# A hybrid encoder trunk on one core: the first loads reordered and halved, one memset for the warm-up, the last products by token halves

## The chip, the core and the metric

The kernel runs on one core of a Trainium2 chip. A core has TensorE (PE, matrix products; PEld is its weight load), VectorE (DVE), ScalarE (ACT), GpSimd (POOL) and SyncE (SP), which here only issues DMAs. The metric is device microseconds of one execution. The kernel before took 1095.82 us, the median of three runs (1095.76 to 1098.31).

## What is computed

Two residual layers over 512 tokens of 1024 features. Layer 0 mixes tokens with a bidirectional gated linear attention, layer 1 with grouped-query softmax attention; each is followed by a gated feed-forward part with a width-3 convolution. An RMS norm stands ahead of each of the four. All inputs and outputs are float32. The stages that the change touches are the first products of layer 0 and the last of layer 1:

```
h = rmsnorm(x, norm_mix[0])
proj = h @ w_in                          # q, k, v, g, r
r_f, r_b = split(r)                      # rank 16 each
log_decay = log_sigmoid(r_dir @ w_up + b_up) / 16
...
x = x + conv_ffn(rmsnorm(x, norm_ffn[1]), ...)   # ends in (silu(gate) * val) @ w_down
```

## The kernel before

**Layout and arithmetic.** `x` is held with features on the partitions: eight chunks `x[c]` of 128 x 512, two to a tile. Every float32 product is three products of a faster type: each operand is split into `hi` (ACT writes a copy, L247 for weights, L373 for inputs) and `lo` (DVE subtracts, L248 and L378), and PE adds `hi*hi`, `hi*lo` and `lo*hi` in one PSUM bank. The RMS factor of a token is multiplied in after the product, so that PE needs only `x` times the norm's weight, not the sums of squares, to begin. Those sums are formed beside (`square`, L380 to L386).

**The beginning.** ACT loads the parameter table `prm` (L302). SP issues 16 DMAs of 256 KB in turn (L307, L308): `x[0]`, the weights of chunk 0, `x[1]`, the weights of chunk 1, and so on. At most eight DMAs are on their way for SP: the ninth waits until the first has landed. DVE fills the two halves of the tile `two` (L320, L321), and eight small products of it (L324) keep PE at work while the loads are under way; what they sum to becomes `halfneg`, the constant -0.5 that an exponent needs later (L326). `gla` then takes `norm.high(0)`, the split of the first weights, whose first half is copied by DVE (L245) and not ACT, and `norm.low(0)` (L488 to L492). The first projection, `seg(0)`, runs `token_steps` (L426 to L444): for each chunk of features there are four token blocks `j`, each with its own PSUM bank, and three products for each. For the first two chunks the products are sorted by operand (L436): four `hi*hi`, then four with the weights' `lo`, then four with the inputs' `lo`. From the third chunk on they go block by block.

**Between.** The sums of squares are turned to token factors `rtok` (L389 to L398), with one step on POOL. PE computes the gate input `rp` (L541) and spreads `rtok` over columns (L349); DVE copies that to `R` (L404) and forms `rf = rp*R` (L545); ACT copies it to `rst` (L547) and DVE corrects 32 of its rows (L548). The gate weights `gst` are copied by ACT (L536) and 32 rows of them corrected by POOL (L537). Products `z` of `gst` and `rst` (L559) stand in PE's order among the products of the second projection `seg(1)`: the first `z` comes after 24 of them. A weight half is brought to SBUF by SP (L169), and copied by ACT into one of four `wh` buffers, of which one holds the gate input's weights `rw` until PE has read them.

**The order.** The code is recorded, and a scheduler sets the order in which the instructions of each engine stand; each engine then works through its own list in order, waiting on semaphores. A small edit can thus move instructions that it doesn't name.

**The end.** The last 24 steps of the list `PLAIN` (L1065 to L1073) sum the last four output chunks, six steps of three products each for a chunk, with all 512 tokens in one PSUM bank. `end` (L1028) adds the bank to `x[c]` on DVE and stores it; for the last chunk it does so by token halves, the first stored through SP, the second through ACT's queue (L1036 to L1038).

Of the kernel before, what the change touches and what calls it, by code (L numbers as in the profile page):

```python
# [8 lines left out]
F32 = mybir.dt.float32  # L9
F32R = mybir.dt.float32r  # L10
U8 = mybir.dt.uint8
AF = mybir.ActivationFunctionType
ALU = mybir.AluOpType

P = 128
S = 512
D = 1024
KC = D // P
NT = S // P
# [5 lines left out]
FC = DFF // P  # L25

SEG_BANKS = (("acc", "acc", "pt", "pt"), ("s", "s", "acc", "acc"), ("acc", "pt", "pt", "s"), ("s", "acc", "acc", "acc"))


GATE_STEPS, GATE_LAG = (1, 3, 5, 7, 10, 12, 15, 17), 2  # L30


# [9 lines left out]
NQ, NPART = 4, 2  # L42
PLAIN = ([(c, k) for c in range(4) for k in range(16, 20)] + [(c, k) for c in range(4) for k in (20, 21)]
         + [(c, k) for c in range(4, 8) for k in range(16, 22)])
# [28 lines left out]
def hybrid_encoder_kernel(  # L73
# [20 lines left out]
    pe, act, dve, pool, sync = nc.tensor, nc.scalar, nc.vector, nc.gpsimd, nc.sync  # L94
    mm = pe.matmul
# [14 lines left out]
    def bank(tag, n):  # L110
        return pp.tile([P, S], F32, tag=tag, bufs=PS[tag], name=nm(n))

    def pair(tag, bufs, dt, n):
        return sp.tile([P, 2 * S], dt, tag=tag, bufs=bufs, name=nm(n))

    def big(dt, n):
        return pair("g", 22, dt, n)

    def tmp(tag, n, w=S):
        return sp.tile([P, w], F32, tag=tag, bufs={"u": 3, "t": 5, "sq": 3}[tag], name=nm(n))  # L120
# [5 lines left out]
    x, x_home = [], []  # L126
# [177 lines left out]
    raw = [pair("raw", NR, F32, "first") for i in range(4)]  # L304
    for c in range(KC):
        r = slice((c % 4) * S, (c % 4 + 1) * S)
        sync.dma_start(x[c], xT[c * P : (c + 1) * P, :])  # L307
        sync.dma_start(raw[c // 2][:, (c % 2) * S : (c % 2 + 1) * S], w_vg[c // 4, :, r])  # L308
    for n in range(4):
        W.loaded[id(w_vg), n // 2, n % 2] = raw[n]  # L310

# [6 lines left out]

    two = tmp("u", "two")
    dve.memset(two[:, :P], 2.0 ** -5)  # L320
    dve.memset(two[:, P : 2 * P], -(2.0 ** -6))  # L321
    warm = bank("po", "warm")
    for i in range(8):
        mm(warm[:, :P], two[:, :P], two[:, P : 2 * P], start=i == 0, stop=i == 7)  # L324
    halfneg = cp.tile([P, 8], F32, name="halfneg")
    dve.tensor_copy(halfneg, warm[:, :8])  # L326
    ones = cp.tile([P, 1], F32, name="ones")
    dve.memset(ones, 1.0 / D)
    bd = cp.tile([P, 2], F32, name="bd")
# [22 lines left out]
    class Norm:  # L352
# [15 lines left out]
        def weight(self, c):  # L368
            return prm[:, PC_NORM + self.idx * KC + c : PC_NORM + self.idx * KC + c + 1]

        def high(self, c):
            t = pair("xhl", 8, F32R, "xhl")
            act.activation(t[:, :S], x[c], AF.Copy, scale=self.weight(c))  # L373
            self.hl[c] = (t[:, :S], t[:, S:])

        def low(self, c):
            hi, lo = self.hl[c]
            dve.scalar_tensor_tensor(lo, x[c], self.weight(c), hi.bitcast(F32), ALU.mult, ALU.subtract)  # L378

        def square(self, c):  # L380
            q = tmp("sq", "sq")
# [24 lines left out]
    def mm3(ps, wh, wl, mh, ml, start, stop):  # L406

        mm(ps, wh, mh, start=start, stop=False)  # L408
        mm(ps, wh, ml, start=False, stop=False)  # L409
        return mm(ps, wl, mh, start=False, stop=stop)  # L410
# [15 lines left out]
    def token_steps(src, i0, hl, ps, width, per_half):  # L426

        for hf in range(KC // per_half):
            wh, wl = W.half(src, i0 + hf)

            late = src is w_vg and i0 > 0 and hf == 0
            for kk in range(per_half):
                todo = [(kk, j, i) for j in range(NT - late) for i in range(3)]
                if late and kk == 1:
                    todo += [(k, NT - 1, i) for k in range(2) for i in range(3)]
                if src is w_vg and i0 + hf * per_half + kk < 2:  # L436
                    todo.sort(key=lambda a: a[2])
                for a, j, i in todo:
                    k, sl = hf * per_half + a, slice(a * width, (a + 1) * width)
                    mm(ps[j][:, :width], hl[k][i == 2][:, j * P : (j + 1) * P], (wl if i == 1 else wh)[:, sl],  # L440
                       start=k == 0 and i == 0, stop=k == KC - 1 and i == 2)
                if kk == 1:
                    W.flush()
                yield  # L444

    def token_tiles(*a):
        for _ in token_steps(*a):
            pass
# [38 lines left out]
    def gla(norm, nxt):  # L487
# [10 lines left out]
        def seg(i, between=None):  # L498
            ps = [bank(tag, "vg") for tag in SEG_BANKS[i]]
            for n, _ in enumerate(token_steps(w_vg, i * 4, norm.hl, ps, S, 2)):  # L500
                if between is not None:
                    between(n)
            return ps
# [318 lines left out]
    def ffn(layer, norm, cw, nxt):  # L822
# [4 lines left out]
        plain = {}  # L827
# [102 lines left out]
        H = S // 2  # L930
# [97 lines left out]
        def end(c, ps):  # L1028
            if nxt is not None or c < KC - 1:
                dve.tensor_tensor(x[c], x[c], ps, ALU.add)  # L1030
                if nxt is not None:
                    nxt.chunk(c)
                else:
                    sync.dma_start(out[c * P : (c + 1) * P, :], x[c])
            else:
                for sl, queue in ((slice(0, S // 2), sync), (slice(S // 2, S), act)):  # L1036
                    dve.tensor_tensor(x[c][:, sl], x[c][:, sl], ps[:, sl], ALU.add)
                    queue.dma_start(out[c * P : (c + 1) * P, sl], x[c][:, sl])  # L1038
# [3 lines left out]
        for m in range(FC):  # L1042
# [15 lines left out]
            else:  # L1058
                for i, y in enumerate(held):
                    t = big(F32R, "gu")  # L1060
# [3 lines left out]
        cur, open_ = None, {}  # L1064
        for u, (c, k) in enumerate(PLAIN):  # L1065
            if u % 8 == 0:
                cur = W.half(w_dn, NPART * NQ * 2 + u // 8)
            sl = slice((u % 8) * P, (u % 8 + 1) * P)
            if c not in open_:
                open_[c] = bank("s" if c == 3 else "acc", "dn")  # L1070
            mm3(open_[c], cur[0][:, sl], cur[1][:, sl], *plain[k], k == 2 * NQ * NPART, k == FC - 1)
            if k == FC - 1:
                end(c, open_[c])  # L1073


    def attention(norm, nxt):
# [116 lines left out]

        ps = [bank("acc" if j < 2 else "pt", "av") for j in range(NT)]
        vg2 = token_steps(w_av, 0, norm.hl, ps, 2 * HD, 4)
        run(qg, 2)
        run(vg2, 1)
# [105 lines left out]
    norms = [Norm(i) for i in range(4)]  # L1303
    cw = gla(norms[0], norms[1])
    ffn(0, norms[1], cw, norms[2])
    attention(norms[2], norms[3])
    ffn(1, norms[3], cw, None)


# [88 lines left out]
```

## Time and profile before

The profiled execution took 1096.11 us, 0.29 us over the median. Its span in the trace is 1094.0 us, so 2.1 us lie around it.

| | busy us | share of the span | instructions |
|---|---|---|---|
| PE | 1086.3 | 99% | 6716 |
| PEld | 975.8 | 89% | 6716 |
| DVE | 870.8 | 80% | 1301 |
| ACT | 683.1 | 62% | 1086 |
| POOL | 126.6 | 12% | 138 |

How to read it: PE's busy time counts matmuls that overlap in the array, so their starts, not their durations, say how fast PE goes. A row of the timeline gives the start and the duration in us, the engine, the line, what is written and read, the number of instructions merged in the row, and in brackets how long the engine had been idle and what released it. Each kernel line Lnnn is a line of the kernel before. Times in the trace count from the start of the span.

### The profile page before, as it was taken

The page shows a single profiled execution, that of the slowest core. Times are in us where ns is not written, and L with a number is a line of the kernel's source. Part 1 is how long each engine was busy: PE and PEld are TensorE (multiplying, and loading weights), DVE is VectorE, ACT ScalarE, POOL GpSimd, SP SyncE. Part 2 cuts the span into 40 slices and gives each one's busy share as a digit, 9 for nine tenths or more (in the row PEclk, how much of TensorE's full clock was granted, in tenths as well). Part 3 has the DMA queues.
Part 4 walks back from the last instruction along what each step waited for, and adds up shares of the span by engine and source line. Part 5 has one row for each costly group of instructions (what it writes and reads, how often), then busy time and mean ns, then how long its engine had stood idle before and what let it go on. Part 6 is the DMA issues. An engine that isn't in the chain of part 4 may idle for free.

```text
span 1094.0 us, 17377 instructions
## 1 busy us (share of the span) xinstructions
PE 1086.3 (99%) x6716; PEld 975.8 (89%) x6716; DVE 870.8 (80%) x1301; ACT 683.1 (62%) x1086; POOL 126.6 (12%) x138
## 2 busy tenths in 40 slices
PE   9999999999999999999999999999999999999998
PEld 7888888888899999999988888788889999999997
DVE  6686776549999899988855578765999889998892
ACT  6565344459775676657664677746977567665660
POOL 0100123022000100010014343002100010001000
PEclk9999999999999999999999999999999999999999
DMA  7323123478634733365757474557944373226542
GB/s 274 133 96 96 58 78 110 139 186 204 152 99 115 155 117 97 95 157 134 248 137 165 122 222 144 169 173 186 216 106 135 98 161 114 101 88 154 135 174 77
DMA packets 52882, 153.76 MB, mean 141 GB/s; under 512 B 6208, under 2 KB 6720, under 8 KB 52800
## 3 DMA queue, kind: packets, MB, share of 16 engines
q1 hardware_dynamic: 36192, 110.56, 31.6%
q0 software_dynamic: 11712, 33.56, 16.9%
q10 hardware_dynamic: 4896, 8.55, 2.1%
q8 instruction: 52, 0.85, 0.3%
q14 instruction: 30, 0.25, 0.1%
HBM read 110.70 MB, written 14.68 MB: 115 GB/s over the span
## 4 chain that ended last, share of the span: by engine, by line
PE 96%; DVE 2%; ACT 1%; DMA 1%; issue 0%; SPq 0%; DVEq 0%; ACTq 0%
PE r L879 37%; PE vg L440 8%; PE op L466 8%; PE up L408 6%; PE up L409 6%; PE up L410 6%; PE dn L409 2%; PE dn L410 2%; PE dn L408 2%; PE av L440 1%; PE o L735 1%; PE A L408 1%; PE A L409 1%; PE A L410 1%; PE B L410 1%; PE B L408 1%
## 5 line engine op out<-in xcount | busy, mean ns | idle before, releaser
L248 DVE TENSOR_TENSOR wl<-raw,wh 128x1024 fp32r<-128x1024 f32 x152 | 185.2, 1220 | 34.1 <-ACT wh L247 33.9
L247 ACT ACTIVATE wh<-raw 128x1024 fp32r<-128x1024 f32 x152 | 158.5, 1052 | 84.4 <-PE op L466 22.6
L879 PE MATMUL r<-gu,wh 128*128 128x256 f32 x896 | 161.8, 283 | 0.0
L879 PE MATMUL r<-xt,wh 128*128 128x256 f32 x832 | 151.2, 283 | 0.0
L879 PEld LDWEIGHTS r<-gu,wh 128*128 128x128 f32 x896 | 140.2, 192 | 0.7
L879 PEld LDWEIGHTS r<-xt,wh 128*128 128x128 f32 x832 | 130.1, 192 | 0.5 <-ACT wh L247 0.2
L879 PE MATMUL r<-gu,wl 128*128 128x256 f32 x448 | 126.6, 283 | 0.0
L879 PE MATMUL r<-xt,wl 128*128 128x256 f32 x416 | 117.4, 283 | 0.0
L879 PE MATMUL r<-nh,wh 128*128 128x256 f32 x312 | 88.9, 285 | 0.7 <-ACT r L907 0.7
L879 PE MATMUL r<-nh,wl 128*128 128x256 f32 x312 | 88.3, 283 | 0.0
L879 PE MATMUL r<-nl,wh 128*128 128x256 f32 x312 | 88.3, 283 | 0.0
L879 PEld LDWEIGHTS r<-gu,wl 128*128 128x128 f32 x448 | 85.9, 192 | 0.0
L440 PE MATMUL vg<-wh,xhl 128*128 128x512 f32 x256 | 79.9, 390 | 1.0 <-DVE wh L245 1.0
L879 PEld LDWEIGHTS r<-xt,wl 128*128 128x128 f32 x416 | 79.7, 192 | 0.0
L409 PE MATMUL up<-nl,wh 128*128 128x512 f32 x192 | 74.9, 390 | 0.0
L408 PE MATMUL up<-nh,wh 128*128 128x512 f32 x192 | 74.9, 390 | 0.0
L410 PE MATMUL up<-nh,wl 128*128 128x512 f32 x192 | 74.7, 389 | 0.0
L466 PE MATMUL op<-oT,wh 128*128 128x512 f32 x256 | 72.1, 394 | 0.0
L879 PEld LDWEIGHTS r<-nh,wh 128*128 128x128 f32 x312 | 59.8, 192 | 3.1 <-ACT r L907 2.9
L879 PEld LDWEIGHTS r<-nl,wh 128*128 128x128 f32 x312 | 59.8, 192 | 0.2
L879 PEld LDWEIGHTS r<-nh,wl 128*128 128x128 f32 x312 | 59.8, 192 | 0.0
L440 PEld LDWEIGHTS vg<-wh,xhl 128*128 128x128 f32 x256 | 47.9, 188 | 11.4 <-ACT sq L382 1.2
(263 smaller groups left out, 2676.8 us busy)
## 6 DMA issues: line engine op xcount, KB each, us to landing
raw<-in_w_up_dram SPq DMA_DIRECT2D x84, 512.0 KB, 4.5
raw<-in_w_down_dram SPq DMA_DIRECT2D x44, 512.0 KB, 3.7
wl<-raw POOLq DMA_DIRECT2D x16, 512.0 KB, 5.2
ring<-p ACTq DMA_DIRECT2D x32, 256.0 KB, 2.7
raw<-in_w_vg_dram SPq DMA_DIRECT2D x12, 512.0 KB, 4.3
wl<-in_w_up_dram POOLq DMA_DIRECT2D x12, 512.0 KB, 7.9
raw<-in_w_kq_dram SPq DMA_DIRECT2D x8, 512.0 KB, 3.6
raw<-in_w_gout_dram SPq DMA_DIRECT2D x8, 512.0 KB, 3.7
```

The costliest lines, as they stand in the source:

```text
L247: act.activation(hi[:, sl], r[:, sl], AF.Copy)
L248: dve.tensor_tensor(lo[:, sl], r[:, sl], hi[:, sl].bitcast(F32), ALU.subtract)
L408: mm(ps, wh, mh, start=start, stop=False)
L409: mm(ps, wh, ml, start=False, stop=False)
L410: return mm(ps, wl, mh, start=False, stop=stop)
L440: mm(ps[j][:, :width], hl[k][i == 2][:, j * P : (j + 1) * P], (wl if i == 1 else wh)[:, sl], start=k == 0 and i == 0, stop=k == KC - 1 and ...
L466: mm(pss[ng][n], wt[:, sl], mv, start=k == 0 and i == 0, stop=k == KC - 1 and i == 2)
L735: last = mm(og[s], l, r, start=False, stop=i == len(parts) - 1, skip_group_check=True)
L879: mm(dst, w[:, sl], m, start=start and j == 0 and a == 0, stop=j == len(pairs) - 1 and a == 2, skip_group_check=True)
```

## The change

The weights of chunk 0 are issued ahead of `x[0]`, which comes in two DMAs of 256 tokens each. `high` and `low` of the first norm work on these halves, and the first 12 products are ordered so that the first two token blocks come first. The tile `two` is filled by one memset and multiplied with itself; the sign and the factor go into the instruction that makes `halfneg`. The last step of `PLAIN` is done for tokens 0 to 255 and then for tokens 256 to 511, in the same bank.

```diff
+WARM = 8
+FIRST = (slice(0, S // 2), slice(S // 2, S))
...
     for c in range(KC):
         r = slice((c % 4) * S, (c % 4 + 1) * S)
-        sync.dma_start(x[c], xT[c * P : (c + 1) * P, :])
-        sync.dma_start(raw[c // 2][:, (c % 2) * S : (c % 2 + 1) * S], w_vg[c // 4, :, r])
+        weights = raw[c // 2][:, (c % 2) * S : (c % 2 + 1) * S], w_vg[c // 4, :, r]
+        if c == 0:
+            sync.dma_start(*weights)
+            for h in FIRST:
+                sync.dma_start(x[c][:, h], xT[c * P : (c + 1) * P, h])
+        else:
+            sync.dma_start(x[c], xT[c * P : (c + 1) * P, :])
+            sync.dma_start(*weights)
...
     dve.memset(two[:, :P], 2.0 ** -5)
-    dve.memset(two[:, P : 2 * P], -(2.0 ** -6))
     warm = bank("po", "warm")
-    for i in range(8):
-        mm(warm[:, :P], two[:, :P], two[:, P : 2 * P], start=i == 0, stop=i == 7)
+    for i in range(WARM):
+        first_mm = mm(warm[:, :P], two[:, :P], two[:, :P], start=i == 0, stop=i == WARM - 1)
     halfneg = cp.tile([P, 8], F32, name="halfneg")
-    dve.tensor_copy(halfneg, warm[:, :8])
+    dve.tensor_scalar(halfneg, warm[:, :8], -4.0 / WARM, None, ALU.mult)
...
+        def parts(self, c):
+            return FIRST if self.idx == c == 0 else (slice(0, S),)
+
         def high(self, c):
             t = pair("xhl", 8, F32R, "xhl")
-            act.activation(t[:, :S], x[c], AF.Copy, scale=self.weight(c))
+            for h in self.parts(c):
+                act.activation(t[:, h], x[c][:, h], AF.Copy, scale=self.weight(c))
             self.hl[c] = (t[:, :S], t[:, S:])
 
         def low(self, c):
             hi, lo = self.hl[c]
-            dve.scalar_tensor_tensor(lo, x[c], self.weight(c), hi.bitcast(F32), ALU.mult, ALU.subtract)
+            for h in self.parts(c):
+                dve.scalar_tensor_tensor(lo[:, h], x[c][:, h], self.weight(c), hi[:, h].bitcast(F32), ALU.mult,
+                                         ALU.subtract)
...
-                if src is w_vg and i0 + hf * per_half + kk < 2:
-                    todo.sort(key=lambda a: a[2])
+                if src is w_vg and i0 == 0 and hf == 0 and kk < 2:
+                    todo.sort(key=lambda a: (a[2] == 2, a[1] >= NT // 2, a[2]) if kk == 0 else a[2])
...
-            mm3(open_[c], cur[0][:, sl], cur[1][:, sl], *plain[k], k == 2 * NQ * NPART, k == FC - 1)
+            if nxt is None and u == len(PLAIN) - 1:
+                for h in (slice(0, H), slice(H, S)):
+                    mm3(open_[c][:, h], cur[0][:, sl], cur[1][:, sl], *(a[:, h] for a in plain[k]), False, h.stop == S)
+            else:
+                mm3(open_[c], cur[0][:, sl], cur[1][:, sl], *plain[k], k == 2 * NQ * NPART, k == FC - 1)
```

## The prediction

> **What bounds the kernel now.** I read the busy time by stretches first, then the chain of waits, then the timelines of the stretches that the change touches. By stretches (start:end, length, then busy us of PE, PEld, DVE, ACT, POOL, the granted clock, DMA share, GB/s):
>
> ```profile
> 40.00:1060.00 1020.00, 1018.09 (x6413) 919.49 (x6412) 832.69 (x1238) 657.60 (x1050) 121.99 (x128) 1.00 0.51 139
> ```
>
> From 40 to 1060 us PE is idle for 1.9 us in all. The change removes no product, so it can only win ahead of the first product and behind the last one. The other side matters more: whatever makes PE wait once, anywhere, is lost, because no later slack gives it back. The chain of waits over the first 30 us says the same (start, us, what):
>
> ```profile
> 1.24 4.16 DMA first<-in_w_vg_dram
> ...
> 5.42 0.44 DVE wh L245
> ...
> 5.99 22.31 PE vg L440 x96
> ```
>
> The first product waits for the weights of chunk 0 (5.40), not for the inputs; then 96 products take 22.31 us.
>
> **The start: an earlier first product, then the same wait.** The timeline of the first 17 us:
>
> ```profile
> 0.81 0.38 SPq L307 DMA_DIRECT2D x<-in_xT_dram  x1
> ...
> 1.24 0.42 SPq L308 DMA_DIRECT2D first<-in_w_vg_dram  x1
> ...
> 1.29 3.69 PE L324 MATMUL warm<-two 128*128 128x128 f32 x16 [1.29 <-DVE bd L330]
> ...
> 1.71 0.42 SPq L307 DMA_DIRECT2D x<-in_xT_dram  x1
> ...
> 3.78 0.72 ACT L373 ACTIVATE xhl<-x,prm 128x512 fp32r<-128x512 f32 x1 [1.25 <-DMA prm<-in_par_dram]
> ...
> 5.99 1.16 PE L440 MATMUL vg<-wh,xhl 128*128 128x512 f32 x4 [1.01 <-DVE wh L245]
> ...
> 7.09 0.33 SPq L307 DMA_DIRECT2D x<-in_xT_dram  x1
> ...
> 7.77 0.33 SPq L308 DMA_DIRECT2D first<-in_w_vg_dram  x1
> ...
> 7.92 2.19 PE L440 MATMUL vg<-wh,xhl 128*128 128x512 f32 x8
> 8.24 0.62 ACT L247 ACTIVATE wh<-first 128x512 fp32r<-128x512 f32 x1
> ...
> 8.91 0.76 PEld L440 LDWEIGHTS vg<-wh,xhl 128*128 128x128 f32 x4 [0.34 <-ACT wh L247]
> ...
> 10.52 0.68 DVE L248 TENSOR_TENSOR wl<-first,wh 128x512 fp32r<-128x512 f32 x1
> ...
> 12.05 0.39 PE L440 MATMUL vg<-wl,xhl 128*128 128x512 f32 x1
> ...
> 16.54 0.71 ACT L373 ACTIVATE xhl<-x,prm 128x512 fp32r<-128x512 f32 x1
> ```
>
> The DMA that is issued first, at 0.81, had landed by 3.78 at the latest, when ACT used it; the second landed at 5.40. With the weights first, DVE's copy is done by about 3.78+0.44 = 4.2. The first half of `x[0]` then lands between 3.8 and 5.4; I take 4.6, half the bytes of the second transfer. ACT's copy of 256 columns lies between nothing and the 0.72 of 512; say 0.45. So the first product starts near 5.1 instead of 5.99, and chunk 0, 12 products of 0.23, ends near 7.9 instead of 8.8 (the second half of `x[0]`, copied by about 6, comes in time).
>
> But chunk 1 doesn't come sooner. SP's issues at 7.09 and 7.77 each waited for `x[1]` and for the weights of chunk 1 to land, so these landed at about 7.07 and 7.75. ACT then works through `x[1]`, its square, and the weights: 8.24+0.62 = 8.86. PE's weight load at 8.91 was waiting for just that. The bytes ahead of these two DMAs are the same after the change, and ACT's order to there too. So the 0.9 us won in chunk 0 becomes a wait of the same length ahead of chunk 1. The price of the extra DMA on their landing is not shown. It is at least nothing, for nothing ahead of them goes away, and at most one issue slot, 1.71-1.24 = 0.47; I take **+0.1**, near nothing, since the DMA engines are behind by then (what was issued at 1.71 landed 5.4 us later). From chunk 2 on PE has slack: its `lo` weights are ready at 11.20 and used at 12.05.
>
> The memset: 128 columns fewer, the eight warm-up products start about 0.13 earlier and PE then waits; the multiply in place of the copy reads the same 128x8. DVE had nothing to do until 5.42. Nothing.
>
> **The end: nothing.** The last products, the adds and the stores, and for the price of 256-column products the chain of waits in a long run of them:
>
> ```profile
> 1090.17 0.39 PE L410 MATMUL dn<-gu,wl 128*128 128x512 f32 x1
> 1090.60 0.75 DVE L1037 TENSOR_TENSOR x<-x,dn 128x256 f32<-128x256 f32 x2 [3.39 <-PE dn L410]
> 1091.05 0.33 SPq L1038 DMA_DIRECT2D out_dram<-x  x1
> 1091.38 0.36 ACTq L1038 DMA_DIRECT2D out_dram<-x  x1
> ```
>
> ```profile
> 855.40 76.31 PE r L879 x636
> ```
>
> Six products of 76.31/636 = 0.12 take 0.72 instead of 3 x 0.23 = 0.69. If the first add could start after three of them, both adds and the last store would come about 0.35 sooner. In the changed kernel's instruction list, though, the first add waits for the last of the six and the second add for nothing new: one wait covers the bank, as before. So 0, or 0.03 later. (The Trainium skill, "PSUM — Partial Sum Buffer", section "PSUM bank collisions raise a hardware error", says that PSUM is to be guarded by bank, not by address, because DVE must not read a bank while PE writes another part of it; this speaks against the edit, and the list agrees. By addresses the sum would be 0.35 lower.)
>
> **What the change moves without naming it.** The two kernels' lists differ in few other places. Two squares come earlier on ACT and push the copies of `x[6]` and `x[7]` back by about one square; the last of these copies was done at 17.25, while PE reaches the last chunk's products 12 x 0.23 ahead of 28.3, at 25.5, so PE's 8 us of other products hide it. One place is tight:
>
> ```
> ACT before: wh L247, gst L536, wh L247, rst L547     after: wh, wh, gst, rst
> DVE before: R L404, rf L545, wl L248, rst L548       after: R, wl, rf, rst
> ```
>
> The rows of before there:
>
> ```profile
> 29.36 1.04 ACT L536 ACTIVATE gst<-graw 128x1024 fp32r<-128x1024 f32 x1
> 31.03 2.39 POOL L537 TENSOR_TENSOR gst<-graw,gst 32x1024 fp32r<-32x1024 f32 x1
> ...
> 32.92 1.06 ACT L247 ACTIVATE wh<-raw 128x1024 fp32r<-128x1024 f32 x1 [2.52 <-PE rp L541]
> ...
> 34.56 0.69 DVE L404 COPY R<-bc 128x512 f32<-128x512 f32 x1
> 35.28 0.69 DVE L545 TENSOR_TENSOR rf<-rp,R 128x512 f32<-128x512 f32 x1
> 35.89 1.22 DVE L248 TENSOR_TENSOR wl<-raw,wh 128x1024 fp32r<-128x1024 f32 x1
> 36.01 0.64 ACT L547 ACTIVATE rst<-rf 128x512 fp32r<-128x512 f32 x1 [2.02 <-DVE rf L545]
> 37.13 0.68 DVE L548 TENSOR_TENSOR rst<-rf,rst 32x512 fp32r<-32x512 f32 x1
> ...
> 38.63 0.40 PE L559 MATMUL z<-rst,gst 128*128 128x512 f32 x1
> ```
>
> `z` needs `rst` (ready at 37.81) and POOL's `gst` (33.42). Both move. ACT's second `wh` waited until 32.92 for the buffer that PE's `rp` products free; now `gst` is queued behind it: 33.98 to about 35.0. POOL starts at about 35.05 and ends at 37.4. On DVE `wl` comes ahead of `rf`: by plain addition `wl` 35.2 to 36.4, `rf` to 37.1, ACT `rst` to 37.75, DVE `rst` to 38.5. `z` would be in time by 0.1 us.
>
> But POOL and DVE now work side by side, where before POOL ran beside DVE work that reads PSUM. The one other place where POOL meets DVE subtractions of two SBUF tiles, each row from its own narrow window:
>
> ```profile
> 107.56 1.12 POOL L636 TENSOR_TENSOR end<-ek,fk 128x384 f32<-128x384 f32 x1 [74.15 <-DVE ek L633]
> 107.92 1.05 DVE L691 TENSOR_TENSOR vrl<-v,vrh 128x256 fp32r<-128x256 f32 x1
> 108.65 1.00 POOL L636 TENSOR_TENSOR end<-ek,fk 128x384 f32<-128x384 f32 x1
> 108.89 1.04 DVE L691 TENSOR_TENSOR vrl<-v,vrh 128x256 fp32r<-128x256 f32 x1
> 109.85 0.74 DVE L691 TENSOR_TENSOR vrl<-v,vrh 128x256 fp32r<-128x256 f32 x2
> ...
> 165.01 2.25 POOL L636 TENSOR_TENSOR end<-ek,fk 128x384 f32<-128x384 f32 x1 [6.98 <-DVE ek L633]
> 165.35 1.22 DVE L248 TENSOR_TENSOR wl<-raw,wh 128x1024 fp32r<-128x1024 f32 x1
> ```
>
> Alone, `vrl` takes 0.74/2 = 0.37. Beside POOL it takes 1.05 and 1.04, and ends 0.29 and 0.28 after POOL does (108.68 and 109.65). At 165 it is the other way: POOL needs 2.25 and DVE's `wl` its usual 1.22. So the two exclude each other, and the one that has begun is let finish. (The Trainium skill, "SBUF — State Buffer", section "SBUF: two separate sides", calls it an exclusive lock of a shared port pair, for the whole instruction, against a DVE operation with two SBUF inputs; these rows agree.)
>
> At 35.05 POOL comes first, by about 0.1, as DVE's `R`, which reads PSUM, ends at 35.25. Then `wl` waits until 37.4 and ends at 38.6, `rf` at 39.2, ACT `rst` at 39.85, DVE `rst` at 40.55, and `z` starts at about 40.65 instead of 38.63: **+2.0 us**. Every start here hangs on PE's `rp`, so the 0.1 from the start adds to it. Bounds of this step: 0 (no exclusion) and 2.5 (POOL's 2.39 stretched by half a us).
>
> **The sum.** 1094.0 span, +0.1 start, +2.0 `z`, 0 end, and 2.1 around the span: 1098.2, to be set against the profiled 1096.11. The median lies 0.29 below that execution: **1097.9 us**, 0.19% over 1095.82. A measurement of this kernel can tell about 0.3% (3.3 us) from no change, so this counts as no change.
>
> **The rivals.**
> *DVE comes first.* If `wl` gets ahead of POOL, as at 165, POOL runs 36.4 to 38.8, `rst` on DVE waits for it until 39.5, and `z` starts at 39.6: +1.0, in all 1096.9. For it: the margin is 0.1. Against: nothing holds POOL back at 35.05.
> *No exclusion here.* POOL's 2.39 is on 32 partitions, and the rows above are on 128. Then `z` is in time: 1095.82+0.1 to +0.2, 1096.0.
> *The early start carries through.* If `x[1]` and its weights land 0.9 sooner with the new order, all of chunk 0's gain stays, and with `z` in time this gives 1094.9. Against it: the same bytes stand ahead of them.
> *A slow clock after the gap (slower).* The warm-up's 16 passes take 3.69, 0.23 each, where the same width later goes faster:
>
> ```profile
> 32.72 0.60 PE L349 MATMUL bc<-ident,rtok 128*128 128x128 f32 x4
> ```
>
> That is at most 0.60/4 = 0.15 each. So PE begins slow, at a guess half as fast, for up to 3.7 us. If the 2.0 us gap ahead of `z` sends it back there, another 3.69/2 = 1.85 us are lost: 1099.8. It decides if a 2 us gap is long enough; the 1.01 gap ahead of 5.99 was not, as 0.23 for 512 columns follows soon. (The Trainium skill, "TensorE: Matmul & The Clock Gate", section "What's actually happening", gives an idle window of about 3.4 us, by which it would not happen and the sum stays at 1097.9; no run here shows it.)
>
> **How the numbers follow.** Chances: forecast 0.55, DVE first 0.18, no exclusion 0.13, early start 0.05, slow clock 0.09. The range leaves out the early start and the slow clock and the lower part of no exclusion. Its upper end has the bounds 0.47 and 2.5 together: 1095.82+3.0 = 1098.8; its lower end is no exclusion with a start 0.2 sooner by scatter: 1095.6. The bound of 0.3% lies at 1099.1 and 1092.5. Faster than that has no case, 0.01; slower has the slow clock and a little of the forecast, 0.11; within, 0.88.
>
> **What would show it.** First product at about 5.1, a wait of PE of about 0.9 ahead of chunk 1, chunk 1 at 8.9 to 9.1; if chunk 1 starts before 8.5, the start is wrong. DVE's first add still after PE's last product, the last store as long after it as now. POOL's `gst` near 35, a `wl` on DVE beside it of 3 us or more, PE idle about 2 us before `z`. If `wl` there shows 1.22, the main step is wrong. If 512-column products after `z` start 0.45 apart, it is the clock.

## The result, and the profile after

The changed kernel took 1099.78 us, the median of 18 runs, beside 1097.34 us for the kernel before in 18 runs. The ratio is 1.002 with a 95% interval of 1.0012 to 1.0028: 2.2 us longer by the ratio and 2.4 by the medians, a difference that is real and lies within the 0.3% that counted as no change. (One of the 18 runs, of 1788.11 us at a granted clock of 0.555, was disturbed and is left out of the ratio.) The profiled executions took 1098.02 us after and 1096.11 us before. So the forecast difference of 2.1 us was close, and the forecast time of 1097.9 us, with its range up to 1098.8, was not: the median lies 1.9 us above it.

**The level.** The 18 runs of before, sorted, have a gap: 8 lie from 1095.76 to 1096.71 and 10 from 1097.32 to 1099.02. The 17 of after do the same, 7 from 1097.84 to 1098.44 and 10 from 1099.50 to 1101.33. I call these the lower and the upper group. Their medians are 1096.10 and 1098.07 before, 1098.02 and 1100.20 after. Between the kernels that is +1.9 in one group and +2.1 in the other. The forecast of 1097.9 is the lower group of after to 0.1 us; the three runs that it was based on had two of the lower group among them.

A time is the span of the trace and what lies around it, and the two moved differently. In the profiled executions 2.1 us lie around the span before and 1.8 after; over the runs the median is 2.1 for before (106 executions with a span on record, 20 of them with 2.8 to 3.35) and 1.74 for after (17). No row of a trace names this part.

**The start.** The chain of waits of after over its first 30 us (start, us, what):

```profile
1.25 3.96 DMA x<-in_xT_dram
...
5.30 0.52 ACT xhl L384
...
5.86 18.36 PE vg L453 x80
```

And the timeline of its first 17 us:

```profile
4.84 0.43 DVE L247 CAST wh<-first 128x512 fp32r<-128x512 f32 x1 [3.50 <-DMA first<-in_w_vg_dram]
...
5.30 0.91 ACT L384 ACTIVATE xhl<-x,prm 128x256 fp32r<-128x256 f32 x2 [2.76 <-DMA x<-in_xT_dram]
...
5.86 0.73 PE L453 MATMUL vg<-wh,xhl 128*128 128x512 f32 x2 [1.02 <-ACT xhl L384]
...
7.77 0.62 ACT L249 ACTIVATE wh<-first 128x512 fp32r<-128x512 f32 x1
7.82 1.99 PE L453 MATMUL vg<-wh,xhl 128*128 128x512 f32 x8
```

The inputs, not the weights, now release the first product. The weights, issued first, are there only at 4.84, and the first half of `x[0]` at 1.25+3.96 = 5.21, where the whole of the second DMA had landed at 5.40 before. So the first product comes at 5.86, 0.13 earlier and not 0.9. The brackets show that PE does not wait for chunk 1 any more: `wh` of chunk 1 is copied at 7.77, and PE goes on.

**Ahead of `z`.** The timeline of after from 28 to 44 us:

```profile
33.52 1.05 ACT L549 ACTIVATE gst<-graw 128x1024 fp32r<-128x1024 f32 x1
...
34.71 2.38 POOL L550 TENSOR_TENSOR gst<-graw,gst 32x1024 fp32r<-32x1024 f32 x1 [4.14 <-issue]
34.79 3.39 DVE L250 TENSOR_TENSOR wl<-raw,wh 128x1024 fp32r<-128x1024 f32 x1
...
38.10 0.68 DVE L558 TENSOR_TENSOR rf<-rp,R 128x512 f32<-128x512 f32 x1
38.81 0.63 ACT L560 ACTIVATE rst<-rf 128x512 fp32r<-128x512 f32 x1 [4.24 <-DVE rf L558]
39.47 0.68 DVE L561 TENSOR_TENSOR rst<-rf,rst 32x512 fp32r<-32x512 f32 x1 [0.69 <-ACT rst L560]
...
40.30 0.47 PE L572 MATMUL z<-rst,gst 128*128 128x512 f32 x1 [1.88 <-DVE rst L561]
```

POOL's `gst` begins at 34.71, 0.08 ahead of DVE's `wl`. That `wl` shows 3.39 us instead of 1.22 and ends at 38.18, 1.09 behind POOL's end at 37.09, nearly its usual length: it stood still until POOL was done. `rf` and `rst` follow one by one, and PE is idle for 1.88 us ahead of `z`. From the first product `rp` to the first `z` it is 40.30-28.59 = 11.71 us, where it was 38.63-28.95 = 9.68 before: 2.0 more. Nothing of that comes back. By stretches, after and then before (start:end, length, busy us of PE, PEld, DVE, ACT, POOL, granted clock, DMA share, GB/s):

```profile
42.00:1062.00 1020.00, 1018.05 (x6414) 919.45 (x6413) 831.24 (x1237) 657.03 (x1049) 121.73 (x128) 1.00 0.52 139
```

```profile
42.00:1062.00 1020.00, 1018.09 (x6413) 919.46 (x6413) 832.79 (x1239) 656.03 (x1047) 121.99 (x128) 1.00 0.51 139
```

**The end.** The timeline of after from its last product on (SPq and ACTq: the queue of SP or ACT, which issues the DMA):

```profile
1092.02 0.28 PE L423 MATMUL dn<-gu,wl 128*128 128x256 f32 x1
1092.34 0.75 DVE L1050 TENSOR_TENSOR x<-x,dn 128x256 f32<-128x256 f32 x2 [3.42 <-PE dn L423]
1092.79 0.33 SPq L1051 DMA_DIRECT2D out_dram<-x  x1
1093.12 0.36 ACTq L1051 DMA_DIRECT2D out_dram<-x  x1
```

The first add starts 0.04 behind the end of the last of the six 256-column products (1092.02+0.28), as it did behind the last 512-column product before; the two stores follow at the same distances. But something has grown behind them. The page begins with the span:

```profile
span 1096.2 us, 17386 instructions
```

From the start of the last store's issue to the end of the span it is 1096.21-1093.12 = 3.09 us after and 1094.03-1091.38 = 2.65 before. So the 2.2 us between the spans are 1.74 at the last store and 0.44 behind it. That store lands 1.75 us after its issue begins in both. Behind the landing, SP works through the rest of a list of waits for the semaphores of all DMAs. The waits that are left from there on, after and then before:

```profile
L1411 SPq EVENT_SEMAPHORE  x8: 27/28/28, 1094.9 to 1095.3; - x8
```

```profile
L1394 SPq EVENT_SEMAPHORE  x1: 28/28/28, 1093.1 to 1093.1; - x1
```

After the change, the last store's semaphore stands early in the list and eight waits follow; before, one. They start 0.06 us apart (0.4 us from the first of the eight to the last), so the seven more are 0.4 us.

### The profile page after: what moved, and what is told of

Its sections match the earlier page's. It is cut to its first block, busy times and chain, and to the rows that moved or that the text cites. A ratio compares the mean times of both kernels' runs of the same rounds, so it can differ in the third digit from the quotient of the medians.

```text
span 1096.2 us, 17386 instructions
## 1 busy us (share of the span) xinstructions
PE 1086.3 (99%) x6719; PEld 976.1 (89%) x6719; DVE 872.5 (80%) x1301; ACT 683.4 (62%) x1087; POOL 126.3 (12%) x138
## 4 chain that ended last, share of the span: by engine, by line
PE 95%; DVE 2%; DMA 1%; ACT 1%; issue 0%; SPq 0%; DVEq 0%; ACTq 0%
PE r L892 37%; PE op L479 8%; PE vg L453 7%; PE up L421 6%; PE up L422 6%; PE up L423 6%; PE dn L421 2%; PE dn L422 2%; PE dn L423 2%; PE av L453 1%; PE o L748 1%; PE A L421 1%; PE A L423 1%; PE A L422 1%; PE B L421 1%; PE B L423 1%
```

## The experiments

**The start alone.** The kernel before with nothing but the loads, the halves and the order of the first 12 products; the memset and the last products stay as they were.

```diff
+            sync.dma_start(*weights)
+            for h in FIRST:
+                sync.dma_start(x[c][:, h], xT[c * P : (c + 1) * P, h])
```

> The kernel before with only the first part of the change: weights of chunk 0 first, x[0] in halves, and the order of the first products; the memset and the last products are as before. Port theory and order theory both: the whole loss comes with this part, since it alone moves gst behind a weight copy on ACT and wl ahead of rf on DVE; z starts 1.9 us after PE is ready for it, the median about 2 us over the kernel before. A rival by which the memset or the last products carry the loss: within 0.5 us of the kernel before, no idle time of PE ahead of z.

It took 1099.69 us beside 1096.58, ratio 1.003 (1.002 to 1.004): the whole loss comes with this part. The timeline of this kernel:

```profile
34.90 2.38 POOL L550 TENSOR_TENSOR gst<-graw,gst 32x1024 fp32r<-32x1024 f32 x1 [4.13 <-issue]
34.99 3.38 DVE L249 TENSOR_TENSOR wl<-raw,wh 128x1024 fp32r<-128x1024 f32 x1
...
40.49 0.47 PE L572 MATMUL z<-rst,gst 128*128 128x512 f32 x1 [1.87 <-DVE rst L561]
```

**`gst` ahead of the weight copies.** The whole change, with ACT's copies of the weights held behind the copy of `gst`, so that POOL gets its work early again.

```diff
-                    act.activation(hi[:, sl], r[:, sl], AF.Copy)
+                    with tc.issue_after(self.behind.ins) if self.behind else ExitStack():
+                        act.activation(hi[:, sl], r[:, sl], AF.Copy)
...
-        act.activation(gst, graw, AF.Copy)
+        W.behind = act.activation(gst, graw, AF.Copy)
```

> The changed kernel, with ACT's copies of weights held behind gst, so that POOL corrects gst early, while DVE reads PSUM. wl still stands ahead of rf on DVE. Port theory: POOL is done by 33, wl there takes 1.22, rst is ready about 0.1 to 0.5 us ahead of z, PE idle ahead of z at most 0.2 us, the time 1.9 us under the changed kernel and 0.3 us under the kernel before. Order theory (wl ahead of rf is the loss by itself): z still more than 1 us late.

It took 1097.24 us beside 1096.58, ratio 1.0005 (0.9995 to 1.0014). The loss is gone; the timeline shows why:

```profile
30.68 2.39 POOL L552 TENSOR_TENSOR gst<-graw,gst 32x1024 fp32r<-32x1024 f32 x1
...
35.41 1.22 DVE L252 TENSOR_TENSOR wl<-raw,wh 128x1024 fp32r<-128x1024 f32 x1
...
38.28 0.40 PE L574 MATMUL z<-rst,gst 128*128 128x512 f32 x1
```

POOL is done at 33.07, the `wl` shows 1.22, and `z` has no bracket: PE did not wait. From the last store to the end of the span it is still 3.08 us, as in the changed kernel.

**A shorter POOL instruction at the same place.** The changed kernel, every instruction in the same order, with POOL's correction cut to 256 of 1024 columns; the correction of the other 768 is left out.

```diff
-        pool.tensor_tensor(gst[64:96, :], graw[64:96, :], gst[64:96, :].bitcast(F32), ALU.subtract)
+        pool.tensor_tensor(gst[64:96, :256], graw[64:96, :256], gst[64:96, :256].bitcast(F32), ALU.subtract)
```

> The changed kernel with POOL's correction of gst cut to a quarter of its columns; the other three quarters of that correction are left out. The order on every engine is that of the changed kernel. Port theory: POOL takes about 0.6 us, wl beside it about 1.5 instead of 3.39, PE idle ahead of z 0 to 0.2 us, time about 1.8 us under the changed kernel. Order theory: nothing changes on DVE's path but POOL's own end, so wl 3.4 or z late by more than 1 us as in the changed kernel.

```profile
36.58 0.73 POOL L550 TENSOR_TENSOR gst<-graw,gst 32x256 fp32r<-32x256 f32 x1 [4.13 <-issue]
36.66 1.73 DVE L250 TENSOR_TENSOR wl<-raw,wh 128x1024 fp32r<-128x1024 f32 x1
...
40.52 0.47 PE L572 MATMUL z<-rst,gst 128*128 128x512 f32 x1 [0.22 <-DVE rst L561]
```

POOL took 1.65 us less, `wl` 3.39-1.73 = 1.66 less, and PE's wait 1.88-0.22 = 1.66 less. The length of POOL's instruction is the price, us for us; the order of the instructions is not. The time, 1097.95 us beside 1096.58 (ratio 1.0007, 0.9998 to 1.0017), agrees.

**Weights first, nothing halved.** The kernel before with its first two DMAs exchanged. Here the scheduler puts `wl` ahead of `rf` on DVE, as in the changed kernel, but leaves ACT's `gst` early.

```diff
+        for a in loads[::-1] if c == 0 else loads:
+            sync.dma_start(*a)
```

> The kernel before with only the order of the first two DMAs turned round: weights of chunk 0 first, x[0] whole. On ACT gst stands ahead of the second weight copy as in the kernel before, on DVE wl stands ahead of rf as in the changed kernel. Port theory: POOL is done by 33.5, wl takes 1.22, z is in time or at most 0.2 us late. Order theory (wl ahead of rf is the loss by itself): z late by 1 us or more. Start: with the weights landing at about 4.8 and all of x[0] at about 5.4, the first product starts at 6.1 to 6.3, and the 96 products end at 28.0 to 28.3 as in the kernel before: the start gives nothing either way.

It took 1097.73 us beside 1097.07, ratio 1.0007 (0.9998 to 1.0016). POOL's `gst` was done ahead of the last `wl`, that `wl` showed 1.22, and `z` waited for nothing, though `rf` stood behind it:

```profile
33.27 2.38 POOL L539 TENSOR_TENSOR gst<-graw,gst 32x1024 fp32r<-32x1024 f32 x1
...
37.39 1.22 DVE L248 TENSOR_TENSOR wl<-raw,wh 128x1024 fp32r<-128x1024 f32 x1
...
40.87 0.40 PE L561 MATMUL z<-rst,gst 128*128 128x512 f32 x1
```

So the order on DVE alone costs nothing. What this run does show is a late beginning: the first product came only at 6.87, when the whole of `x[0]`, issued second, had landed and was copied.

```profile
6.87 1.38 PE L442 MATMUL vg<-wh,xhl 128*128 128x512 f32 x4 [2.10 <-ACT xhl L375]
```

**Two banks at the end.** gst_first, with the last chunk's 18 products done as 36 of 256 columns in two PSUM banks, so that the first add needs only the first bank.

```diff
+                banks = [open_[c], bank("s", "dn")]
+                for h, ps in zip((slice(0, H), slice(H, S)), banks):
...
+                        mm3(ps[:, h], cur[0][:, w], cur[1][:, w], *(a[:, h] for a in plain[16 + i]), i == 0, i == 5)
```

> The changed kernel with gst first on ACT (as gst_first) and the last output chunk summed token half by token half, each half in a bank of its own. DVE's add of the first half then waits for its own products alone. 36 products of 256 columns take 0.12 each, 4.2 us instead of 15 of 512 and 6 of 256, 4.1: 0.1 us more. The first add and store lie wholly beside PE; the second add begins right behind the last product instead of 0.37 us later. Theory that one wait covers the bank: the last store is issued 0.35 to 0.4 us after the last product's end less than now, net 0.25 to 0.3 us under gst_first. Rival, that the add of a half can't be had sooner or that the end hangs on something else: no difference from gst_first.

```profile
1088.41 0.42 DVE L1053 TENSOR_TENSOR x<-x,dn 128x256 f32<-128x256 f32 x1 [1.46 <-PE dn L425]
...
1088.86 0.33 SPq L1054 DMA_DIRECT2D out_dram<-x  x1
...
1090.57 0.42 DVE L1053 TENSOR_TENSOR x<-x,dn 128x256 f32<-128x256 f32 x1 [1.73 <-PE dn L425]
1091.02 0.36 ACTq L1054 DMA_DIRECT2D out_dram<-x  x1
```

The first add now starts 2.16 us ahead of the second: with two banks the wait is split, with one it was not. But the last store starts at 1091.02, where it started at 1090.93 in gst_first, with `z` at the same place in both to 0.01. The last product ends 0.42 us later here. Some 0.2 of that are the added 256-column products; the rest lies ahead of the last chunk, whose first product starts at 1086.06 instead of 1085.84. From there to the last store it is 4.96 us here and 5.09 in gst_first, so the split gains 0.13 us in these traces, and the times don't show it: 1096.28 us beside 1097.07 (ratio 0.9999, 0.999 to 1.0008) is that of before.

**The changed kernel again**, with a trace that fell in its upper group:

> The changed kernel, for a second trace. Port theory: POOL's gst at about 34.7, wl beside it 3.3 to 3.4, PE idle 1.9 ahead of z. If the trace falls in the upper group of times, the first products are slow in it (0.43 us each up to about 9 us) by the theory of the clock.

It took 1099.89 us beside 1097.07, ratio 1.0018 (1.0009 to 1.0027); the traced execution took 1100.13. PE's wait ahead of `z` was 1.9 again. New is the beginning of its timeline:

```profile
5.97 1.22 PE L453 MATMUL vg<-wh,xhl 128*128 128x512 f32 x2 [1.03 <-ACT xhl L384]
...
6.98 1.05 PE L453 MATMUL vg<-wl,xhl 128*128 128x512 f32 x2
...
7.84 1.05 PE L453 MATMUL vg<-wh,xhl 128*128 128x512 f32 x2
```

Rows of two products start 0.86 apart, so a product takes 0.43 us, not the 0.23 of later ones; this goes on until about 10.4. The chain of waits gives 24.13 us for the first 96 products, which other traces do in 22.0.

**The kernel before, four times more:** once with its time measured in ten runs, three times with one execution each.

> The kernel before, a second time, for a second trace of it. If the spread of its executions (1095.76 to 1099.02) lies at the start, the first product of chunk 1 starts at another time than 8.9 us, or the first products go slower; if at the end, the way from DVE's last add to the end of the span is not 3.4 us; otherwise it lies between, as idle time of PE or as a lower granted clock.

> The kernel before once more, for one trace beside its own time. The theory that the first products of some executions run slowly: either 96 products of vg from about 5.95 for 22.0 to 22.3 us and a profiled execution of 1096.0 to 1096.6, or their spacing is 0.43 instead of 0.23 for the first eight to ten, the 96 take 23.6 to 24.1, and the profiled execution shows 1097.5 to 1098.5. The rival, a wait elsewhere (the ring's DMA ahead of attention's transposes, 2.0 us in one trace): 22.0 to 22.3 at the start and 1097.5 or more in all.

> As the one ahead of it, the kernel before a further time: start of 22.0 to 22.3 us for 96 products and about 1096.3 in all, or 23.6 to 24.1 and about 1098. The rival: a long execution with a fast start.

> The kernel before once more, one trace beside its own time, to find one of its executions of 1097.2 us or more in a trace. If the clock at the start makes the difference: the 96 first products take 23.6 to 24.1 us in such a one and 22.0 to 22.3 in one of 1095.5 to 1096.9. If another place does: 22.0 to 22.3 in both.

before_again took 1097.54 us beside 1096.58, ratio 1.0004 (0.9995 to 1.0013): the same kernel, and its median moved by 1 us. The single executions took 1096.81, 1095.77 and 1097.65. The chains of waits of the fourth and the fifth:

```profile
5.92 22.02 PE vg L440 x96
```

```profile
6.31 23.61 PE vg L440 x96
```

The fifth is of the upper group of before, and its 96 products took 1.6 us more. Its timeline has the same slow beginning:

```profile
6.31 2.04 PE L440 MATMUL vg<-wh,xhl 128*128 128x512 f32 x4 [1.24 <-DVE wh L245]
8.15 1.80 PE L440 MATMUL vg<-wl,xhl 128*128 128x512 f32 x4
9.80 1.99 PE L440 MATMUL vg<-wh,xhl 128*128 128x512 f32 x8
```

The first eight products take 9.80-6.31 = 3.49 us, 0.44 each, and the next eight about 0.23 each. So both kernels show it. Over all runs of before here, 124, the lower group has 61 with a median of 1096.09 and the upper 63 with 1097.92, divided at 1097.1. The times alone have no gap there, because what lies around the span varies; the spans have one: of the 106 on record, 54 lie from 1093.3 to 1094.6 and 52 from 1095.1 to 1096.9, with medians of 1093.9 and 1095.7.

**A longer warm-up.** gst_first, and the kernel before, with 12 warm-up products instead of 8, so that PE has no gap ahead of the first product.

```diff
-WARM = 8
+WARM = 12
```

> gst_first with twelve warm-up products in place of eight, so that PE has no gap between them and the first product. All kernels so far show two groups of times about 1.7 us apart. Theory that the upper group are executions in which PE's clock comes up later, and the first products go at 0.43 us each instead of 0.23 (as in the trace of gst_quarter): with no gap the clock is up sooner or more surely, and the upper group shrinks; the lower group is 0 to 0.8 us later than in gst_first since the last warm-up products stand ahead of the first product. Rival (the groups come from elsewhere): the same two groups with the same shares.

> Twelve warm-up products again, no gap ahead of the first product. If the late clock at the start comes from the gap of one us, the 96 products take 22.0 here too, as in the first trace (21.92). If the clock comes up late whatever stands ahead, half of such traces show 23.6 or more. If the ring's DMA wait belongs to this kernel, PE waits 2.0 us for it again ahead of pt; if it was a chance event, 0.2.

> The kernel before with twelve warm-up products instead of eight, and nothing else. With the clock theory: 96 products in 21.9 to 22.1 us from about 6.1, and times in one group near 1096.3 to 1096.8. With the rival (groups from elsewhere): two groups 1.8 us apart as before, whatever the start shows.

The times: 1100.03 us beside 1097.07 (ratio 1.0025, 1.0016 to 1.0033), one execution of 1097.65, and 1099.73 beside 1096.80 (ratio 1.0021, 1.001 to 1.0033). So this is worse, and the two groups did not go: the eleven runs of the first lie at 1097.95 to 1098.06 and at 1099.68 to 1101.79. In two of the three traces no product was at half speed, in gst_first_warm12_again only the first; from the end of the warm-up, at 6.16, 6.65 and 6.48, the 96 took 21.92, 22.04 and 21.84 us. In the first of them PE lost its time elsewhere, in attention, as its timeline shows:

```profile
702.33 0.44 PE L1277 MATMUL pt<-ident,ring 128*128 128x128 f32 x3 [1.97 <-DMA ring<-p]
```

That wait for the ring's DMA was 2.0, 0.9 and 0.8 us in these three traces, and 0.2 in gst_first, at most 0.7 in any other trace. No trace of their upper groups was taken, but each run has its mean granted clock on record: 0.998 in all 13 runs of the upper groups (from 1099.56 up), 0.999 or 1.0 in the other eight. All 106 runs of before show 1.0. So the upper times with the longer warm-up are of another kind than those of before; in which stretch their clock was low isn't shown.

**One DMA more, elsewhere.** The kernel before with other inputs in halves: `x[7]` alone, `x[5]` to `x[7]`, or all eight.

```diff
-        sync.dma_start(x[c], xT[c * P : (c + 1) * P, :])
+        for h in (slice(0, S // 2), slice(S // 2, S)) if c == 7 else (slice(0, S),):
+            sync.dma_start(x[c][:, h], xT[c * P : (c + 1) * P, h])
```

> The kernel before with x[7], the last of the first inputs, loaded in two DMAs: one DMA more, none of it near the first product. In the traces so far the span ends 2.59 to 2.70 us after the start of the last store's issue in every kernel with 16 first loads, and 3.06 to 3.12 in every kernel with 17. If the DMA's number does that (each DMA takes the next of eight semaphores, so one more shifts which of them the last stores use): 3.06 to 3.12 here too. If the halves of x[0] or the changed first products do it: 2.6 to 2.7.

> As before_split1, with x[5], x[6] and x[7] in two DMAs each, three DMAs more. If each DMA more costs 0.43 behind the last store: 3.9. If only the position among eight semaphores counts: any value between about 2.6 and 3.6, not bound to grow with the number. If neither: 2.6 to 2.7.

> As before_split1, with all eight inputs in two DMAs each, eight DMAs more: once round the eight semaphores. If only the position counts: 2.59 to 2.70 as before, with the last stores on the same semaphores. If each DMA more costs 0.43: 6.1. If any halving costs 0.43 once: 3.06 to 3.12.

The last store and the page's first line, of before_split1 and then of before_split8:

```profile
1095.33 0.36 ACTq L1039 DMA_DIRECT2D out_dram<-x  x1
```

```profile
span 1098.4 us, 17381 instructions
```

```profile
1091.42 0.36 ACTq L1039 DMA_DIRECT2D out_dram<-x  x1
```

```profile
span 1094.1 us, 17392 instructions
```

The end takes 3.07 us with one DMA more, 3.03 with three (1096.3-1093.27), 2.68 with eight. So it isn't each DMA, nor any halving, but where the number leaves the last stores among the eight semaphores that DMAs take in turn. SP's list of waits shows it again: behind the landing of the last store there follow eight waits with one DMA more, six with three, and one with eight more, as in the kernel before. From that landing to the end of the span it is 1.34, 1.21 and 0.92 us, and 0.90 to 0.97 in the traces of before. Over all 19 traces the last store lands 1.74 to 1.79 us after its issue, whatever the kernel, and only the waits behind it differ.

There is a surprise in the first two: before_split1 and before_split3 have the whole loss ahead of `z`, though nothing at the start was changed. The waits of PE in before_split1:

```profile
PE z L560 <- DVE rst L549: 1.9, 1, 1.9
```

The single executions took 1100.51, 1098.27 and 1095.78. So with 17 or 19 first loads the scheduler turned `gst` and the weight copy round, whether the halves were of `x[0]` or of the last inputs; with 16 and 24 it did not.

**The position put back in the changed kernel.** gst_first with `x[1]` to `x[7]` in halves too, eight DMAs more than before.

> gst_first with x[1] to x[7] loaded in two DMAs each as well: eight first loads more than the kernel before, once round the eight semaphores. If the 0.43 behind the last store goes with the position: the span ends 2.6 to 2.7 us after the start of the last store's issue instead of 3.07, and the executions with a fast start come to 1095.6 to 1095.8 instead of 1096.1 to 1096.2, unless the seven added issues (0.4 each on SP) make the first loads late. If the halves of x[0] or the changed products do it: 3.07 and 1096.1. PE without a wait ahead of z in either case.

It took 1096.46 us beside 1097.71, ratio 0.999 (0.9981 to 0.9999). The span ends 1095.4-1092.76 = 2.64 us after the last store's start. Its lowest four of eleven runs lie at 1095.09 to 1095.78, those of gst_first at 1096.08 to 1096.19. About 0.4 of the 0.7 us between these groups is in the spans; the rest lies around the span (a median of 1.7 us here, 2.1 in gst_first), which no row names. This is the one version that comes out below the kernel before, by some 0.1%, less than the 0.3% that I hold a measurement of this kernel to.

## Why the prediction was right about the difference and wrong about the time

**The step that failed** is the last line of the sum: "The median lies 0.29 below that execution: 1097.9 us". Three runs were taken for the level of the kernel. Its level is two levels, 1.8 us apart (1096.09 and 1097.92), of about equal share; the profiled execution and two of the three runs were of the lower one. The median of many runs falls in the gap or on either side of it: 1097.34, 1096.58, 1097.07, 1096.80 and 1097.71 in the five sets of before. After, the median lies 1.76 us above the profiled execution of 1098.02, where the sum put it 0.29 below: 2.05 us of error in this one step, all of the miss of 1.9 and a little more. The range had room for the price of `z` and of the DMA, and none for this. One of the three runs shown, 1098.31, was 2.5 us over the other two; that was the sign.

The sum ahead of that step, 1098.2 for the profiled execution, came out at 1098.02, and this is partly luck: it had three terms wrong by 0.3 to 0.5 us each, and these errors cancel in part, as the last paragraph of this section shows.

**What makes the levels** was in the prediction as a rival, at the wrong place. "A slow clock after the gap" was expected behind the 2 us gap ahead of `z`. There the chain of after goes on at 4.35/19 = 0.23 us a product, so nothing is lost:

```profile
40.30 0.47 PE z L572
40.77 4.35 PE vg L453 x19
```

Of the gap ahead of the first product the prediction said that it "was not" long enough, from one trace. In five of 19 traces (after_again, before_fifth, before_split1, gst_first_split8, gst_quarter) PE began at half speed there, for the first seven to ten products. The clock column doesn't tell them: the stretch of after_again in which its products are 0.43 apart reads

```profile
5.00:10.00 5.00, 4.03 (x10) 3.16 (x11) 4.44 (x9) 4.59 (x9) 0.00 (x0) 1.00 1.00 347
```

with a granted clock of 1.00 in the column after POOL's. (The Trainium skill, "TensorE: Matmul & The Clock Gate", section "What's actually happening", says that TensorE begins at half rate, that some 3.4 us of activity release it, and that the window by which this is judged runs free, so that the number of half-speed products differs from run to run. The traces agree: 0.43 and 0.23 us a product, and a warm-up of 3.5 to 3.8 us that is enough in some executions and not in others. That the window's phase decides is not shown here.)

weights_first is a sixth, of another kind. Its first three products go at full speed, then seven follow at 0.43 us each, and here the clock column of the same stretch does tell it:

```profile
5.00:10.00 5.00, 3.13 (x9) 2.54 (x10) 3.96 (x8) 3.91 (x7) 0.00 (x0) 0.77 1.03 350
```

In its trace the granted clock is 0.50 for 3.41 us from 7.71 on, which loses 1.7 us; this begins 0.84 us behind the end of the gap of 2.10 us ahead of the first product. So what the rival feared does occur, but behind the gap of 1.88 ahead of `z` it didn't in any of the five traces that have one. That the longer gap is the cause isn't shown: of weights_first's ten runs three have a mean clock of 0.998, as this one, and seven 1.0.

The six traces belong to upper times (before_split1, with one execution, has no group to compare), and of the other 13 traces none with a group does. This shows what goes with the upper times in five of five; why the clock is late or falls in an execution stays open. For the longer warm-up the granted clock of 0.998 points to the second kind, without a trace.

**The start**, +0.1: right in that the earlier product brings nothing to speak of, wrong in its working. The weights landed at 4.8, not by 3.8, and the half of `x[0]` at 5.2, not at 4.6; the sizes were taken from how `x[0]` had landed, and weights issued first took as long as weights issued second. So there was no 0.9 to be lost ahead of chunk 1, and no wait there. In traces with an early clock the products `rp` start at 28.60 to 28.95 in the kernel before (mean of four 28.78) and at 28.59 to 28.78 in four with the changed start (28.65): 0.1 won.

**`z`**, +2.0: right, in the mechanism and the size. From `rp` to `z` it took 2.0 more, PE's wait was 1.88, POOL began at 34.71 ("near 35"), `wl` took 3.39 ("3 us or more"). gst_quarter shows that POOL's time is the price and weights_first that the order on DVE isn't. That the rows were on 128 partitions and this one on 32 made no difference.

**The end**, 0: right for the wait that covers the bank, and for its price: a first add 0.04 behind the last product. Two banks show that the bank is what counts.

**The extra DMA**, bounds 0 to 0.47: looked for at the first loads, found behind the last store. Over all traces, with the spans to two digits, the end took 2.64 to 2.71 us in the seven with 16 first loads, 3.08 or 3.09 in the nine with 17, 3.00 with 19, and 2.66 and 2.67 with 24. The sum had no term for it.

So in the two profiled executions the spans differ by -0.36 up to `rp`, +2.03 from there to `z`, +0.07 from `z` to the last store, and +0.44 behind it: 2.18, where the sum had 0.1, 2.0 and 0. The start that came out 0.46 lower and the end that was not in the sum cancel; and the part around the span, taken as 2.1, was 1.8. With the start at the -0.1 of the mean the spans would be 2.4 apart, as the medians of the lower groups are (1096.3 and 1093.9).

## What to carry to other kernels

Set a forecast against the level of many runs, and where the few that there are lie 2 us apart, find out what the kernel's times do before a sum of 2 us is put on one of them. Where instructions are ordered by a scheduler, compare the whole lists before and after: here one more DMA among the first loads moved a POOL instruction beside a DVE one 30 us later, and that was most of the change's price; it also moved the last store ahead in the list of waits at the end, which was 0.4 us more. An instruction on POOL that reads SBUF belongs where DVE works from PSUM or is idle; beside a DVE operation with two SBUF inputs one of them stood still here until the other was done (3.39 us instead of 1.22).

## What was not expected of the hardware

The 0.4 us at the end of the program that go with the DMAs' number: SP's waits, 0.06 us each, and how many of them stand behind the last store (one with 16 or 24 first loads, eight with 17, six with 19). That a first DMA of 256 KB of weights takes 4.0 us from its issue at 0.81 to 4.84, and a DMA of half the bytes issued behind it landed at 5.21. That a longer warm-up, which did bring the clock up by the second product in all three traces, came with longer times: the first product came 0.1 to 0.4 us later (6.01 and 6.30 beside 5.88 in gst_first, 6.28 beside 5.99), the ring's DMA in attention, 700 us on, kept PE waiting for 0.8 to 2.0 us, and the mean granted clock of the longer runs was 0.998. Whether the warm-up brings the last two about isn't shown.
